# Mixer A's values: from eight narrow blocks inside the attention to three wide groups of seven half-sized products ahead of it

## The chip, the cores and the metric

One NeuronCore of one Trainium2 chip runs the whole program. The metric is the device time of one execution in microseconds (us). The kernel before takes 1451.91 us, the median of three runs (1451.7 to 1453.12).

## The reference

A two-layer encoder trunk on x of 512 positions by 1024, all in float32. Layer 0 mixes tokens with mixer A, layer 1 with mixer B (multi-head latent attention); each mixer is followed by a squared-ReLU MLP of width 4096. Mixer A is what the change touches:

```
qkv = (rms_norm(x) @ w_qkv).reshape(512, 3, 3 groups, 8 heads, 128)
for g, (window, dilation) in enumerate(((128, 1), (512, 4), (2048, 16))):
    q, k = rope(rms_norm(qkv[:, 0, g])), rope(rms_norm(qkv[:, 1, g]))
    v = qkv[:, 2, g]                       # 512 x 1024 for each g
    o_g, lse_g = dilated_window_attention(q, k, v)
o = sum_g softmax_g(lse)[g] * o_g
x = x + o @ w_o
```

So the values are three products of the 512 x 1024 activation with a 1024 x 1024 weight, one for each group.

## The kernel before, in words

**Split precision.** Each float32 weight tile comes by DMA into `raw` and is split into a high part `whi` (a copy on ScalarE, L157) and a low part `wlo` (a subtraction on VectorE, L158). The activation `hT` is split in the same way when the normalised input is transposed (L212 to L221). Each tile product is three TensorE matmuls: high by high, high by low, low by high (L184 in `run_block`). A block over 1024 of depth and 512 rows is thus 8 x 4 x 3 = 96 matmuls, into four PSUM banks named `acc`.

**Mixer A** goes by pairs of heads, b = 0 to 3. For a pair:

- `qk_block(b, g)` for g = 0, 1, 2: 96 matmuls of 512 columns (q and k of two heads). Each bank is then squared and summed on ScalarE (`junk`, L136), rotated and scaled on VectorE (L308, L311, L315, L316), transposed on TensorE (`tp`, L123), copied to `qkT` (L325). Scores follow (`sc`, L340, L344, L351), the masks from `ca`, the maximum (L359) and the exponentials (L362).
- `v_block(b, h)` for both heads: 96 matmuls of 384 columns (the three groups of one head), copied on ScalarE to `vt` (L369). Group 0 goes through a DRAM tile `vd` and comes back in two other layouts, `v0n` and `v0c`.
- `merge`: two small products `scm` (L386, L411) with a chain of small VectorE and ScalarE steps around them weigh the three groups; the weights are multiplied into the probabilities `P` (L417).
- `pv`: the probabilities are transposed (L123), copied to `pT` (L426 on VectorE, L433 on ScalarE), and multiplied with the values into `sco` (L440, L444), which goes to `oT` (L446).

In the last pair the values of one head stand ahead of the qk blocks, and those of the other after the merge. Then comes the output projection, whose first 72 matmuls need only the first heads.

**The order on each engine** comes from a scheduler that simulates the program and arranges each engine's instructions. Every engine works strictly through its own list, so an instruction that waits holds up all behind it on its engine.

**The MLPs** already use seven half-sized products per block (`wino`): a 512 x 1024 x 1024 product cut into quarters, with sums of quarters of the activation (`S`, then its split `asp`, L485 and L486) and of the weights (`wqs`), where the sum of two weight quarters is made by a DMA from GpSimd's queue that adds into SBUF (L509). A product is 24 matmuls of 512 columns (L580). `ORDER` sets their sequence: products 1, 5, 3, 6, 2, 7, 4. In the last block of an MLP (`done` given) the finished rows go on to mixer B's norm or to the output.

GpSimd has short tensor operations too, among them the tables `cgB` and `sgB` of mixer B (L691 to L693), which wait for the DMA of the gain `gr`.

Of the kernel before, what the change touches and what calls it, by code (L numbers as in the profile page):

```python
# [10 lines left out]
F32 = mybir.dt.float32  # L11
F32R = mybir.dt.float32r
AF = mybir.ActivationFunctionType
ALU = mybir.AluOpType
# [73 lines left out]
def encoder_kernel(ctx: ExitStack, tc: tile.TileContext, x, norm_mix, norm_ffn, a_w_qkv, a_q_gain, a_k_gain,  # L88
# [151 lines left out]
    oT = x16.tile([P, HA, S], F32, tag="x16", name="oT")  # L240
    with tc.tile_pool(name="apool", bufs=1, reuse_waits="tile") as ap_, \
            tc.tile_pool(name="aw", bufs=2, reuse_waits="tile") as aw, \
            tc.tile_pool(name="adram", bufs=2, space=bass.MemoryType.DRAM) as ad:
        cosg = [ap_.tile([P, NT, 2, DH], F32, name=f"cosg{g}") for g in range(NG)]
        sing = [ap_.tile([P, NT, 2, DH], F32, name=f"sing{g}") for g in range(NG)]
        xts = [aw.tile([P, D], F32, tag="vt", name=nm("xt")) for r in range(2)]
        xts += [ap_.tile([P, D], F32, tag=t, name=nm("xt")) for t in ("P00", "gqk")]

        def load_x(r):
            for hf in range(2):  # L250
                nc.sync.dma_start(xts[r][:, 512 * hf:512 * hf + 512], x_v[:, r, 512 * hf:512 * hf + 512])

        def load_w0(k):
            early[("first", k)] = load_raw(*qk_units(0, 0)[k], 512)
        cas = ap_.tile([P, 2176], F32, name="ca")
        ca = cas[:, 0:C_ALL - C_KEEP]
        load_x(0)
        gain_b = gain_table(norm_mix[0:1, :].rearrange("o d -> (o d)"), D, "g_mix0")
        nc.sync.dma_start(ck[:, 0:P], consts[:, 0:P])
        load_w0(0)  # L260
# [4 lines left out]
        load_x(3)  # L265
        nc.sync.dma_start(ca[:, 0:C_M1 - C_KEEP], consts[:, C_KEEP:C_M1])
        nc.sync.dma_start(ca[:, C_M1 - C_KEEP:], consts[:, C_M1:C_ALL])
        nc.sync.dma_start(ck[:, P:C_KEEP], consts[:, P:C_KEEP])
        for r in range(NT):
            norm_tile(r, xts[r], gain_b, hT, aw, xn_tag="qkT")  # L270
        gqk0 = ap_.tile([P, 2, 512], F32, tag="gqk", name="gqk")
# [3 lines left out]
        cosA = cc(C_COSA, C_SINA).rearrange("p (r d) -> p r d", r=NT)  # L275
        sinA = cc(C_SINA, C_M1).rearrange("p (r f d) -> p r f d", r=NT, f=2)
# [4 lines left out]
        def tables(g):  # L281

            gqk = gqk0 if g == 0 else aw.tile([P, 4, DH], F32, tag="t1", name=nm("gq"))
            for t, src in enumerate((a_q_gain, a_k_gain)):
                nc.sync.dma_start(gqk[:, t, 0:DH], src[0, g].partition_broadcast(P))
            for t in range(2):
                gb = gqk[:, t, 0:DH].rearrange("p (f d) -> p f d", f=2).unsqueeze(1)
                gb = gb.broadcast_to([P, NT, 2, 64])
                V.tensor_tensor(cosg[g][:, :, t].rearrange("p r (f d) -> p r f d", f=2),
                                cosA.unsqueeze(2).broadcast_to([P, NT, 2, 64]), gb, op=ALU.mult)  # L290
                V.tensor_tensor(sing[g][:, :, t].rearrange("p r (f d) -> p r f d", f=2), sinA, gb, op=ALU.mult)

        def qk_block(b, g, Pt, stats, first):

            qkT = aw.tile([P, 4, S], F32, tag="qkT", name=nm("qkT"))

            def evac(r, acc):
                a4 = acc.rearrange("p (c d) -> p c d", c=4)
                a5 = acc.rearrange("p (t h d) -> p t h d", t=2, h=2)
                ss = st.tile([P, 8], F32, tag="qss", name=nm("qss"))  # L300
                junk = aw.tile([P, P], F32, tag="junk", name=nm("junk"), bufs=1)
                for c in range(4):
                    mean_square(junk, a4[:, c], DH, ss[:, c:c + 1])
                t1 = aw.tile([P, 4, DH], F32, tag="t1", name=nm("t1"))
                t2 = aw.tile([P, 4, DH], F32, tag="t2", name=nm("t2"))
                t15 = t1.rearrange("p (t h) d -> p t h d", t=2)
                t25 = t2.rearrange("p (t h) d -> p t h d", t=2)
                V.tensor_tensor(t15, a5, cosg[g][:, r].unsqueeze(2).broadcast_to([P, 2, 2, DH]), op=ALU.mult)  # L308
                for hf in range(2):
                    o_ = 64 - hf * 64  # L310
                    V.tensor_tensor(t25[:, :, :, hf * 64:hf * 64 + 64], a5[:, :, :, o_:o_ + 64],  # L311
                                    sing[g][:, r, :, o_:o_ + 64].unsqueeze(2).broadcast_to([P, 2, 2, 64]),
                                    op=ALU.mult)
                rs = rstd_of(ss[:, 0:4], 4, EPS, "qrs")
                V.tensor_tensor(t1, t1, t2, op=ALU.add)  # L315
                V.tensor_tensor(t1, t1, rs.unsqueeze(2).broadcast_to([P, 4, DH]), op=ALU.mult)  # L316
                tp = tp_p.tile([P, 512], F32, tag="tp", name=nm("tp"))
                for c in range(4):
                    transpose(tp[:, c * P:(c + 1) * P], t1[:, c])
                tv = tp.rearrange("p (c t) -> p c t", c=4)  # L320
                if g == 0:
                    dst = qkT.rearrange("p c (m r) -> p c m r", r=NT)[:, :, :, r]
                else:
# [624 lines left out]
```

## Time and profile before

| what | value |
|---|---|
| median of three runs | 1451.91 us |
| time of the profiled execution | 1451.78 us |
| span of its profile | 1449.6 us, so 2.18 us lie around the span |
| mean granted clock of TensorE | 0.999 |
| TensorE matmul busy | 97% of the span, 7116 matmuls |
| VectorE, ScalarE, GpSimd busy | 61%, 50%, 14% |

A row of a group says: line, engine, operation, the tiles written and read, the count, then busy time and mean ns of one. A row of the timeline says: start, duration, engine, line, operation, and in brackets the idle time ahead of it and what ended it. In the chain of waits a row is a stretch of the chain that ended last. Matmuls overlap, so their single durations add up to more than the time that passes; the time from the start of one stretch to the next is what counts.

### The profile page before, as it was taken

Reading aid. Unit: us, or ns where it says so; the run is one execution under the profiler, and the core shown is the slowest. Engines: PE = TensorE matmul, PEld = TensorE weight load, DVE = VectorE, ACT = ScalarE, POOL = GpSimd, SP = SyncE. Lnnn points to the kernel's source line nnn. Section 1 sums busy time; section 2 is a strip of 40 time slices with the busy share of each in tenths; the row PEclk is TensorE's granted clock in tenths of the full one; section 3 lists DMA queues with packets and bytes.
Section 4 is the critical chain, followed back from the end, with each engine's and each line's share of the span. In section 5 each row is a group of like instructions: output and inputs, shape, how many; then the busy total and the mean of one; then the engine's idle time right before and its main releaser. Section 6 shows DMA issues by size and latency. Waiting matters only on the chain.

```text
span 1449.6 us, 19315 instructions
## 1 busy us (share of the span) xinstructions
PE 1410.4 (97%) x7116; PEld 1196.8 (83%) x7116; DVE 887.1 (61%) x1421; ACT 727.2 (50%) x1590; POOL 198.4 (14%) x197
## 2 busy tenths in 40 slices
PE   7999999999999999999999999899999999999998
PEld 6889889889988878888888877776768988888877
DVE  6765566566537655266475749788755266475647
ACT  5544455355335533453544545777633454544543
POOL 1120120011011101011020222332101011020210
PEclk9999999999999999999999999999999999999999
DMA  7325114321622344749394853310013749394853
GB/s 228 100 57 162 58 49 129 110 63 45 174 92 62 97 140 141 222 112 236 91 233 127 195 136 66 99 30 30 30 44 136 206 111 239 93 223 138 189 116 88
DMA packets 134813, 177.52 MB, mean 122 GB/s; under 512 B 8768, under 2 KB 73536, under 8 KB 134720
## 3 DMA queue, kind: packets, MB, share of 16 engines
q1 hardware_dynamic: 117312, 142.74, 31.1%
q0 software_dynamic: 17408, 33.56, 14.0%
q8 instruction: 56, 0.92, 0.2%
q14 instruction: 37, 0.30, 0.1%
HBM read 172.07 MB, written 4.19 MB: 122 GB/s over the span
## 4 chain that ended last, share of the span: by engine, by line
PE 89%; ACT 4%; DVE 3%; DMA 2%; issue 1%; POOL 1%; SPq 0%; DVEq 0%; ACTq 0%; POOLq 0%
PE acc L184 58%; PE sc L580 10%; PE tp L580 7%; PE tp L123 4%; PE acc L859 1%; PE acc L835 1%; PE sc L753 1%; PE sco L444 1%; PE sco L440 1%; PE sc L351 1%; PE sc L835 1%; ACT whi L157 1%; ACT junkb L136 1%; DVE wlo L158 1%; PE tp L859 0%
## 5 line engine op out<-in xcount | busy, mean ns | idle before, releaser
L184 PE MATMUL acc<-whi,hT 128*128 128x512 f32 (+2 forms) x1600 | 486.3, 379 | 5.6 <-DVE t L311 2.2
L158 DVE TENSOR_TENSOR wlo<-raw,whi 128x1024 fp32r<-128x1024 f32 (+3 forms) x170 | 195.7, 1156 | 230.5 <-ACT whi L157 229.5
L184 PEld LDWEIGHTS acc<-whi,hT 128*128 128x128 f32 x1600 | 296.2, 189 | 47.3 <-issue 2.9
L184 PE MATMUL acc<-hT_f,whi 128*128 128x512 f32 (+1 forms) x1152 | 319.4, 366 | 1.9 <-DVE resid L641 1.2
L157 ACT ACTIVATE whi<-raw 128x1024 fp32r<-128x1024 f32 (+3 forms) x170 | 170.0, 1005 | 269.0 <-PE acc L184 177.4
L184 PE MATMUL acc<-wlo,hT 128*128 128x512 f32 (+2 forms) x800 | 300.2, 375 | 0.2 <-DVE wlo L158 0.2
L184 PEld LDWEIGHTS acc<-hT_f,whi 128*128 128x128 f32 x1152 | 208.4, 189 | 37.8 <-DVE resid L641 1.6
L524 DVE TENSOR_TENSOR wlo<-wqs,whi 128x1024 fp32r<-128x1024 f32 x112 | 137.3, 1227 | 113.6 <-ACT whi L523 113.5
L184 PE MATMUL acc<-hT_f,wlo 128*128 128x512 f32 (+1 forms) x576 | 205.1, 365 | 0.0
L523 ACT ACTIVATE whi<-wqs 128x1024 fp32r<-128x1024 f32 x112 | 118.6, 1060 | 167.6 <-PE acc L184 66.2
L184 PEld LDWEIGHTS acc<-wlo,hT 128*128 128x128 f32 x800 | 151.2, 189 | 20.5 <-DVE wlo L158 1.1
L580 PE MATMUL sc<-whi,asp 128*128 128x512 f32 x512 | 165.1, 390 | 0.8 <-ACT asp L485 0.8
L509 POOL DMA_DIRECT2D wqs<-in_ffn_w_dram x64 | 77.6, 1350 | 528.4 <-DVE wlo L524 339.9
L184 PEld LDWEIGHTS acc<-hT_f,wlo 128*128 128x128 f32 x576 | 108.6, 189 | 17.5
L131 POOL TENSOR_TENSOR qrs<-rs_v,nhalf 128x4 f32<-128x4 f32 x48 | 61.5, 1290 | 408.3 <-DVE rs_v L128 393.8
L580 PE MATMUL tp<-whi,asp 128*128 128x512 f32 x352 | 112.2, 390 | 2.6 <-DVE asp L486 2.6
L580 PEld LDWEIGHTS sc<-whi,asp 128*128 128x128 f32 x512 | 96.1, 188 | 21.6 <-ACT asp L485 1.6
L580 PE MATMUL sc<-wlo,asp 128*128 128x512 f32 x256 | 99.6, 389 | 0.0
L580 PEld LDWEIGHTS tp<-whi,asp 128*128 128x128 f32 x352 | 65.9, 188 | 17.2 <-DVE asp L486 3.5
L580 PE MATMUL tp<-wlo,asp 128*128 128x512 f32 x176 | 68.5, 389 | 0.0
L136 ACT ACTIVATE junk<-acc 128x128 f32<-128x128 f32 x192 | 53.1, 277 | 18.9 <-PE acc L184 13.8
L554 DVE TENSOR_TENSOR resid<-resid,sc 128x512 f32<-128x512 f32 x64 | 43.0, 682 | 24.4 <-PE sc L580 24.4
(190 smaller groups left out, 1796.3 us busy)
## 6 DMA issues: line engine op xcount, KB each, us to landing
wqs<-in_ffn_w_dram SPq DMA_DIRECT2D x80, 512.0 KB, 5.1
raw<-in_ffn_w_dram SPq DMA_DIRECT2D x64, 512.0 KB, 4.4
wqs<-in_ffn_w_dram POOLq DMA_DIRECT2D x64, 512.0 KB, 7.2
raw<-in_a_w_qkv_dram SPq DMA_DIRECT2D x96, 256.0 KB, 3.4
raw<-in_a_w_qkv_dram SPq DMA_DIRECT2D x64, 192.0 KB, 2.8
raw<-in_a_w_o_dram SPq DMA_DIRECT2D x8, 512.0 KB, 4.0
raw<-in_b_w_o_dram SPq DMA_DIRECT2D x8, 512.0 KB, 3.7
xt<-in_x_dram SPq DMA_DIRECT2D x8, 256.0 KB, 5.7
```

What stands on the lines that cost most here:

```text
L123: PE.transpose(o, i, ident)
L131: G.tensor_tensor(out, v[:, :n], nhalf[:, :n], op=ALU.pow)
L136: A.activation(junk, x, AF.Square, scale=1.0 / math.sqrt(dim), accum_out=out)
L157: A.activation(hi[:, :nk, :n], raw[:, :nk, :n], AF.Copy)
L158: V.tensor_tensor(lo[:, :nk, :n], raw[:, :nk, :n], hi[:, :nk, :n].bitcast(F32), op=ALU.subtract)
L184: PE.matmul(accs[o][:, oc], lhsT=lt, rhs=rt, start=(kt == 0 and p_i == 0 and hv == 0), stop=(kt == total - 1 and p_i == 2), skip_group_che ...
L509: nc.gpsimd.dma_start(t, src, accum_op=ALU.add)
L523: A.activation(hi, x, AF.Copy)
L524: V.tensor_tensor(lo, x, hi.bitcast(F32), op=ALU.subtract)
L554: V.tensor_tensor(sl, sl, banks[t], op=op)
L580: PE.matmul(bk[t], lhsT=lt, rhs=rt[:, j], start=(first and k == 0 and i_ == 0), stop=(k == 3 and i_ == 2), skip_group_check=True)
L835: PE.matmul(sc, lhsT=lt, rhs=rt, start=(i == 0), stop=(i == 4))
```

## The change

- A new `v_phase` stands right behind the first qk block (pair 0, group 0). For each group it makes all 1024 value columns by seven half-sized products in the sequence 1, 2, 5, 3, 6, 7, 4, as 24 matmuls of 512 columns each (3 x 7 x 24 = 504). The results collect in `vo` and go to a DRAM tile `vall` per group; `v_load` brings what a pair needs back, ten DMAs per pair.
- The weights come as whole quarters (`b11`, `b21`, `b12`, `b22`, `bT`). Their sums are made by adding DMAs on GpSimd's queue (four sums for group 0, two for groups 1 and 2) and otherwise by VectorE.
- The sums of activation quarters `Ssp` (four of them) are made once, from the unsplit copies `h32` and `stg`, while the input is normalised.
- The eight `v_block`s, their `vt` copies and the round trips through `vd` go. The qk blocks follow one another, with the first block's q and k tables read from `rot` and the masks `ca` loaded after the value phase. The buffer `qkT` alternates between two pools.
- In the last block of each MLP product 2 moves from fifth to second place (`ORDER_LAST`).

```
+    def v_phase(vp):
+        h32 = vp.tile([P, 2, KD, P], F32, name="h32")
...
+        def add_block(t, g, ki, ni):
+            for u in range(2):
+                nc.gpsimd.dma_start(t[:, 2 * u:2 * u + 2], wblk(g, ki, ni, u), accum_op=ALU.add)
...
+                A.activation(stg[0, i], tvs[0], AF.Copy)
+                V.tensor_tensor(stg[1, i], h32[:, i, 0:4], stg[0, i], op=ALU.subtract)
+                V.tensor_tensor(stg[0, i], stg[0, i], tvs[1], op=ALU.subtract)
...
+        qk_proj(0, 0, qkT0, first_homes, lambda: jk, first=True)
+        def split_s(n, x, i):
+            hi, lo = (Ssp[n][:, :, c, i * P:(i + 1) * P] for c in range(2))
+            A.activation(hi, x, AF.Copy)
+            V.tensor_tensor(lo, x, hi.bitcast(F32), op=ALU.subtract)
...
+        def product(p, w, banks, first, u, t, parts):
+            if (p, u) not in parts:
+                parts[p, u] = split_w(w[:, 2 * u:2 * u + 2])
+            hi, lo = parts[p, u]
+            for j in range(2):
+                k = 2 * u + j
+                ah, al = A_OF[p](k, 0, t), A_OF[p](k, 1, t)
+                for i_, (lt, rt) in enumerate(((ah, hi), (ah, lo), (al, hi))):
+                    PE.matmul(banks[t], lhsT=lt, rhs=rt[:, j], start=(first and k == 0 and i_ == 0),
+                              stop=(k == 3 and i_ == 2), skip_group_check=True)
...
+            for p, w, bk in ((1, b11, ba), (2, b21, bd)):
+                for u, t in ALONE:
+                    product(p, w, bk, True, u, t, parts)
+            put(0, 0, "set", ba, False)
+            put(0, 0, "add", bd, True)
+            for u in range(2 if g else 0):
+                us = slice(2 * u, 2 * u + 2)
+                V.tensor_tensor(bT[:, us], b11[:, us], b12[:, us], op=ALU.add)
+            bb = new_banks("b")
+            for u, t in ALONE:
+                product(5, bT, bb, True, u, t, parts)
+            put(1, 1, "set", bb, False)
+            add_block(bT, g, 1, 1)
...
+            for u, t in ALONE:
+                product(6, bT, ba, False, u, t, parts)
+            put(0, 1, "sub", ba, True)
+            add_block(bT, g, 1, 0)
...
-        def v_block(b, h, vd):
-            vt = aw.tile([P, NT, NG, DH], F32, tag="vt", name=nm("vt"))
...
-            units = [(w7[:, k:k + 2, 2, :, 2 * b + h, :], 2, NG) for k in range(0, KD, 2)]
-            run_block(units, [1] * 4, 384, act_stationary(hT, 384), evac)
...
-                qk_all()
-                vs = [v_all(0), v_all(1)]
-                merge(stats, Pt, False)
...
+            vs = v_load(b)
+            for g in range(NG):
...
+                scores(b, g, qkT, Pt, stats)
+            merge(stats, Pt)
...
-        for p, chain, first, (i, n, op) in ORDER:
+        for p, chain, first, (i, n, op) in ORDER if done is None else ORDER_LAST:
...
+    ORDER_LAST = [ORDER[0], ORDER[4]] + ORDER[1:4] + ORDER[5:]
```

What this moves, at three places. A name with a number is a tile and its buffer.

**VectorE, the start of the program.** Before, as the last rows of the input are split (`hT`) and the first qk block is rotated (`t`):

```order
L221 TENSOR_TENSOR hT_91<-tp_212,hT_91 128x4x128
L221 TENSOR_TENSOR hT_91<-tp_219,hT_91 128x4x128
L308 TENSOR_TENSOR t_59_296<-acc_243,cosg_104 128x512
L311 TENSOR_TENSOR t_60_297<-acc_243,sing_107 128x4x64 x2
L128 TENSOR_SCALAR rs_v_301<-qss_290 128x4
L308 TENSOR_TENSOR t_66_343<-acc_244,cosg_104 128x512
L311 TENSOR_TENSOR t_67_344<-acc_244,sing_107 128x4x64 x2
```

The same place now, where the last bank of the same block (`t_61`) is done only thirty-odd rows further on (`h_109` is the copy `h32`):

```order
L355 TENSOR_TENSOR stg_210<-h_109,stg_210 128x512
L356 TENSOR_TENSOR stg_210<-stg_210,tp_203 128x512
L267 TENSOR_TENSOR t_46_296<-acc_247,cosg_103 128x512
L270 TENSOR_TENSOR t_46_296<-acc_247,sing_104 128x4x64 x2
L128 TENSOR_SCALAR rs_v_300<-qss_291 128x4
L370 TENSOR_TENSOR Ssp_114<-stg_210,Ssp_114 128x4x128
L370 TENSOR_TENSOR Ssp_112<-stg_210,Ssp_112 128x4x128
L274 TENSOR_TENSOR t_46_296<-t_46_296 128x512
L128 TENSOR_SCALAR rs_v_345<-qss_336 128x4
L374 TENSOR_TENSOR stg_210<-stg_210,h_109 128x512
L275 TENSOR_TENSOR t_46_296<-t_46_296,qrs_302 128x512
L346 TENSOR_TENSOR hT_91<-tp_222,hT_91 128x4x128
```

The sums `stg` and their splits `Ssp` now stand between the steps of the qk block. On TensorE the transposes of `t_61` stand ahead of the first matmul of product 5.

**TensorE, `pv` of the first pair.** Before, between the values (`sco`) and the transposes of the probabilities (`tp`), with matmuls of the pair's value and next qk blocks (`acc`) in between:

```order
L440 MATMUL sco_1352<-pT_1329,vt_999 128x128
L440 MATMUL sco_1352<-pT_1336,vt_999 128x128
L184 MATMUL acc_1428<-whi_1495,hT_91 128x512
L184 MATMUL acc_1429<-whi_1495,hT_91 128x512
L184 MATMUL acc_1429<-wlo_1496,hT_91 128x512
L184 MATMUL acc_1429<-whi_1495,hT_91 128x512 x2
L184 MATMUL acc_1429<-wlo_1496,hT_91 128x512
L444 MATMUL sco_1352<-pT_1343,v0n_1133 128x4x32
L123 MATMUL tp_1370<-ck,P_230 128x128 x2
```

Now, at the same place:

```order
L610 MATMUL sco_1934<-pT_1911,vt_1314 128x128
L610 MATMUL sco_1934<-pT_1918,vt_1314 128x128
L123 MATMUL tp_1920<-ck,P_1305 128x128 x4
L123 MATMUL tp_1927<-ck,P_1305 128x128 x4
L614 MATMUL sco_1934<-pT_1925,v0n_1317 128x4x32
L123 MATMUL tp_1952<-ck,P_1308 128x128 x4
L614 MATMUL sco_1934<-pT_1932,v0c_1318 128x4x32
L614 MATMUL sco_1934<-pT_1925,v0n_1317 128x4x32
```

From the second `scm` to the last `sco` no matmul of a qk block stands among them any more, in this pair and the next two.

**TensorE, the end of the last pair's scores.** Before, around the first of the two merge products (`scm`), with matmuls of the output projection (`acc`):

```order
L184 MATMUL acc_4990<-whi_4993,hT_4858 128x512
L184 MATMUL acc_4990<-wlo_4994,hT_4858 128x512
L386 MATMUL scm_4681<-ca,xsel_4678 128x4 x4
L184 MATMUL acc_4987<-whi_4993,hT_4858 128x512 x2
L184 MATMUL acc_4987<-wlo_4994,hT_4858 128x512
L184 MATMUL acc_4988<-whi_4993,hT_4858 128x512 x2
```

Now:

```order
L184 MATMUL acc_4738<-whi_4801,hT_4606 128x512
L517 MATMUL sc_4548<-qkT_4327 128x128
L517 MATMUL sc_4560<-qkT_4327 128x128
L517 MATMUL sc_4548<-qkT_4327 128x128
L517 MATMUL sc_4560<-qkT_4327 128x128
L555 MATMUL scm_4575<-ca,xsel_4572 128x4 x4
L580 MATMUL scm_4596<-ca,xsel_4572 128x4 x2
L123 MATMUL tp_4607<-ck,P_3800 128x128 x4
```

The 72 matmuls of the projection now all stand ahead of the last scores, and nothing stands between the last scores and the two merge products.

More of the change, by code (lines that the diff above doesn't have):

```diff
@@ L293, in qk_block @@
[L293 to L323, printed above, removed]
-                    dst = qkT[:, :, r * P:(r + 1) * P]
-                A.activation(dst, tv, AF.Copy)
-            run_block(qk_units(b, g), [4] if first else [1] * 4, 512, act_stationary(hT, 512), evac,
-                      name="first" if first else None)
```

248 lines of the change are left out of this document (190 added, 58 removed).

## The prediction

> **What bounds the kernel now.** I read the page's busy times first, then the chain of waits for the whole run.
>
> ```profile
> PE 1410.4 (97%) x7116; PEld 1196.8 (83%) x7116; DVE 887.1 (61%) x1421; ACT 727.2 (50%) x1590; POOL 198.4 (14%) x197
> PE 89%; ACT 4%; DVE 3%; DMA 2%; issue 1%; POOL 1%; SPq 0%; DVEq 0%; ACTq 0%; POOLq 0%
> ```
>
> TensorE works almost all the time, and 89% of the chain that ended last is its own work. So each microsecond of matmuls taken away counts, unless something else then ends late. What that could be is read stage by stage. The table by stage says where TensorE already waits in mixer A:
>
> ```profile
> 30.00:80.00 50.00, 50.00 (x252) 42.04 (x251) 38.38 (x76) 31.35 (x110) 10.47 (x9) 1.00 0.27 83
> 80.00:130.00 50.00, 47.76 (x273) 45.58 (x272) 29.96 (x52) 23.96 (x70) 6.00 (x4) 0.97 0.37 106
> 130.00:180.00 50.00, 50.00 (x288) 43.84 (x287) 29.07 (x56) 19.61 (x50) 4.37 (x4) 1.00 0.28 84
> 480.00:530.00 50.00, 46.56 (x272) 42.26 (x271) 35.54 (x67) 26.61 (x77) 4.84 (x4) 1.00 0.35 107
> ```
>
> The columns are TensorE, its weight loads, VectorE, ScalarE and GpSimd busy, then the granted clock. TensorE has no gap in the middle pairs; VectorE is busy for 29 to 38 us of 50. It has room on the average, but the first 50 us of real work (30 to 80) leave it only 11.6.
>
> **1. The matmuls of the values.** The pitch of a matmul is the length of an unbroken stretch in the chain of waits over its count. A stretch of value blocks alone (384 columns), and one of 512 columns:
>
> ```profile
> 117.82 14.56 PE acc L184 x84
> 841.40 18.83 PE acc L184 x83
> ```
>
> That is 14.56/84 = 0.1733 us and 18.83/83 = 0.2269 us. Removed: 8 blocks x 96 = 768 matmuls, 768 x 0.1733 = 133.1 us. Added: 504 x 0.2269 = 114.4 us. Difference **-18.7 us**, all of it on the engine that sets the end. [...]
>
> **2. The start.** The new sums and splits of activation quarters and the splits of the value weights stand on VectorE among the first qk block's steps, and the transposes of that block's last bank stand on TensorE ahead of product 5. VectorE's pitch of a 512-wide step, a 1024-wide split and the rest is read here:
>
> ```profile
> 10.47 1.23 DVE L158 TENSOR_TENSOR wlo<-raw,whi 128x1024 fp32r<-128x1024 f32 x1 [1.65 <-ACT whi L157]
> 11.61 0.68 DVE L221 TENSOR_TENSOR hT<-tp,hT 128x512 fp32r<-128x512 f32 x1
> ...
> 18.53 1.28 DVE L221 TENSOR_TENSOR hT<-tp,hT 128x512 fp32r<-128x512 f32 x2
> ...
> 32.09 0.75 DVE L311 TENSOR_TENSOR t<-acc,sing 128x256 f32<-128x256 f32 x2
> 32.76 0.16 DVE L128 TENSOR_SCALAR rs_v<-qss 128x4 f32<-128x4 f32 x1
> ```
>
> Start to start, a split takes 1.14 us and a pair of L311 0.67; of two 512-wide steps in 1.28 us the second adds 0.60. From the split that begins at 18.53 (its place in the list is the same in both) up to the last step of that bank the new list has 38 steps of 512, four pairs, nine splits, one normalisation (about 1.2) and small ones (0.6): 22.8 + 2.7 + 10.3 + 1.8 = 37.6 us. So the bank is done at 56.1 us at the earliest, if VectorE never waits. TensorE meanwhile has 144 matmuls of 512 columns and 11 groups of transposes to do. Before, it had done as many here:
>
> ```profile
> 49.87 0.44 PE tp L123 x4
> 50.31 0.70 PE acc L184 x3
> ```
>
> That is at 51.0, so it would stand idle for 5.1 us or more. VectorE waits now and then for ScalarE and GpSimd, so I take **+6.0** (5 to 9). This also says what covers the sums: nothing does, VectorE has no slack here.
>
> **3. Inside the value phase.** A product takes 24 x 0.2269 = 5.4 us of TensorE. VectorE needs two splits and two or three result steps, 2.3 + 1.2 to 1.8 us, so it keeps up, and ScalarE (two copies of 1.06) too. Groups 1 and 2 add four 1024-wide sums (4.6 us per group) ahead of products 5 and 7. The adding DMAs are priced by the page's row of such transfers (count, size, us to landing):
>
> ```profile
> wqs<-in_ffn_w_dram POOLq DMA_DIRECT2D x64, 512.0 KB, 7.2
> ```
>
> The sum for product 6 is issued behind the split for 5 and needed 10.9 us after 5 begins, with 3 between; the MLPs run these three in the same sequence without a wait on TensorE that shows. At a group's change a quarter arrives behind the last splits of the group before. **+2.5** for all three groups: the lower bound is 0 (the MLPs), the upper 6.8, a split's 1.14 at each of two changes of group and ahead of 5 and 7 in two groups; I take two to three of these six, since the sums are queued among splits that run one product ahead.
>
> **4. `pv` of the first three pairs without matmuls to fill it.** The last pair of before is the nearest row, for there hardly any stand in it:
>
> ```profile
> 521.99 0.50 PE L411 MATMUL scm<-ca,xsel 128*128 128x4 f32 x4
> 525.75 0.66 PE L123 MATMUL tp<-ck,P 128*128 128x128 f32 x4 [2.09 <-DVE pT L426]
> 532.23 0.66 PE L123 MATMUL tp<-ck,P 128*128 128x128 f32 x4 [0.29 <-DVE pT L426]
> ```
>
> In the pairs before it the same steps have cover: the window 130 to 180 shows TensorE busy throughout. Each of three pairs takes on 2.09 + 0.29 = 2.4 us: **+7.2**. Below, 0 if the scaling of `P` is done in time; above 13.8, if the six matmuls that still stood in the second head (1.2) and one result wait (1.0) come on top in each.
>
> **5. The last pair's merge.** The first product of the merge waits for the maxima of the last scores, the second for exponentials and weights. Before, VectorE and ScalarE went through this chain under matmuls of the projection and the last value block:
>
> ```profile
> 503.54 1.05 PE L351 MATMUL sc<-qkT 128*128 128x128 f32 x8
> 504.41 1.29 DVE L356 TENSOR_TENSOR P<-sc,ca 128x512 f32<-128x512 f32 x2 [1.01 <-PE sc L351]
> 505.62 0.68 DVE L656 TENSOR_TENSOR hT<-oT,hT 128x512 fp32r<-128x512 f32 x1
> ...
> 506.81 0.68 DVE L656 TENSOR_TENSOR hT<-oT,hT 128x512 fp32r<-128x512 f32 x1
> ...
> 508.01 1.89 DVE L656 TENSOR_TENSOR hT<-oT,hT 128x512 fp32r<-128x512 f32 x3
> 510.01 0.40 ACT L362 ACTIVATE P<-P,stat 128x128 f32<-128x128 f32 x1 [1.71 <-DVE stat L360]
> 513.11 1.05 ACT L157 ACTIVATE whi<-raw 128x1024 fp32r<-128x1024 f32 x1
> 514.06 0.21 ACT L397 ACTIVATE me<-me 128x24 f32<-128x24 f32 x1
> 514.19 1.23 DVE L158 TENSOR_TENSOR wlo<-raw,whi 128x1024 fp32r<-128x1024 f32 x1 [1.77 <-ACT whi L157]
> 516.40 0.49 DVE L406 TENSOR_TENSOR xsel<-me,ca 128x128 f32<-128x128 f32 x2
> ```
>
> From the end of the scores (504.6) to the second product's operand (516.9) it took 12.3 us. Five L656 steps (3.0) ahead of the exponentials and a copy and a split of weights (2.1) behind them lay within; without these it is 7.2. Now all of it stands open, since the projection's 72 matmuls come ahead of it: **+8** (7.2 to 12.3), nearer to the lower end because those L656 steps are needed by the 72 matmuls and so are done before.
>
> **6. The clock.** After the one idle time of over 2 us in the middle of mixer A the granted clock falls:
>
> ```profile
> 93.67 0.41 PE L184 MATMUL acc<-whi,hT 128*128 128x384 f32 x1 [2.24 <-DVE t L311]
> 95.00:100.00 5.00, 5.00 (x21) 5.00 (x20) 5.00 (x10) 1.10 (x5) 2.93 (x2) 0.66 0.54 150
> ```
>
> 21 matmuls ran there in 5 us, against 5/0.1733 = 29 at the full pitch, so 1.4 us are lost. After the 2.09 us at 525.75 nothing is lost that the profile shows. The open stretch of part 5 is longer than either: **+1.5**, with 0 to 6 should `pv` and the start lose it too. [...]
>
> **7. The last block of the MLPs.** In layer 0 GpSimd's adding DMAs for product 6 now stand behind `cgB` and `sgB`, which wait for `gr`:
>
> ```profile
> 860.25 3.62 DMA gr<-in_b_q_gain_dram
> ...
> 872.89 6.32 DMA wqs<-in_ffn_w_dram
> ```
>
> ```profile
> 875.20 1.26 POOL L509 DMA_DIRECT2D wqs<-in_ffn_w_dram  x1
> ```
>
> ```profile
> 865.00:870.00 5.00, 3.50 (x15) 2.55 (x15) 5.00 (x6) 1.06 (x1) 5.00 (x6) 1.00 0.01 2
> 870.00:875.00 5.00, 4.57 (x20) 3.49 (x19) 4.92 (x5) 4.01 (x4) 5.00 (x5) 1.00 0.15 6
> ...
> 895.00:900.00 5.00, 3.98 (x22) 3.14 (x21) 4.95 (x6) 2.55 (x4) 0.56 (x2) 1.00 0.00 0
> ```
>
> Before, the tables held up DMAs of product 4 alone, and TensorE lost 1.5 + 0.4 + 1.0 = 3 us in this stage. Now both DMAs of product 6 go out at 875.2, land 6.3 later and are copied (1.1) by 882.6, while TensorE, which ends its last L184 stretch at 860.2 and has products 2, 5 and 3 ahead (16.3), is there at 876.5: it waits 6.1. The difference is 3, and some of it comes back since products 7 and 4 then find all ready: **+2** (0 to 5). In layer 1 no such tables stand in the way. Product 5's operand came late after product 1:
>
> ```profile
> 1412.92 0.73 PE L580 MATMUL tp<-whi,asp 128*128 128x512 f32 x2 [1.14 <-DVE asp L486]
> ```
>
> Product 2 needs no sum and fills that time: **-1.5** (-3 to 0). The removed `vt` copies, the `vd` round trips and the later `ca` load lie under matmuls and count nothing; the ten loads of `v_load` have a pair's 90 us to land.
>
> **The sum.** -18.7 + 6.0 + 2.5 + 7.2 + 8 + 1.5 + 2 - 1.5 = **+7.0 us**. The profiled execution took 1451.8 (its span of 1449.6 and 2.2 around it), 0.1 under the median, so the change gives 1451.8 + 7.0 = **1458.8 us**. With all bounds low: -18.7 + 5 + 0 + 0 + 7.2 + 0 + 0 - 3 = -9.5; with all high +34.
>
> **The rivals.** A measurement can tell about 0.2% (2.9 us) from no change.
>
> *Saved matmuls carry through: faster.* The point is VectorE's lateness in `pv`. If the scheduler's neighbours leave the scaled `P` ready, part 4 is 1 instead of 7.2, and the value phase has no waits (0). Then -18.7 + 5.5 + 0 + 1 + 7.2 + 0 + 1 - 2 = -6.0, so 1446. For it: `P` for groups 1 and 2 is scaled before group 0. Against it: the 2.09 us of the last pair came in this order too.
>
> *No change.* Part 4 at half (3.6), part 2 at 5, the clock and layer 0 at nothing: -18.7 + 5 + 2 + 3.6 + 8 - 1 = -1.1, so 1450.7.
>
> *Adding DMAs late: much slower.* If the sums for products 6 and 4 land late in each group, TensorE stops six times. The second half's split for 5 ends 2.3 us after 5 begins, its sum lands 7.2 later and is split by 11.8; it is needed at 13.6. A landing of 11 would be 2 late, six times +12 on the forecast, so 1471. For it: at the start the DMA engines are at their fullest. Against it: the MLPs show no such wait.
>
> **How the numbers follow.** The forecast's case has 0.44, the faster rival 0.26, no change 0.18, late DMAs 0.12. Within the forecast's case nearly all lies over +2.9. So faster 0.26, within 0.2% 0.18, slower 0.56. The range takes in the faster rival and part of the late DMAs, **1445 to 1470 us**; the forecast's own case is 1455 to 1465.
>
> **What would show it.** In the changed profile: matmuls of the value phase at 0.227 us; an idle time of 5 us or more ahead of product 5 (about 50 to 57 us) that ends with a rotated `t`; waits for `pT` of 2 us in each pair; an open 7 to 12 us at the last pair's `scm` with a fallen clock behind it. If `pv` of the middle pairs shows no idle time, or the start keeps TensorE busy, the kernel is faster and the forecast wrong.

## The result, and the profile after

The changed kernel takes 1464.07 us (median), the kernel before in the same comparison 1451.81. The ratio is 1.008, with a 95% interval of 1.006 to 1.010: slower by 0.8%, 12.3 us. Forecast were 1458.8 us, slower with 0.56, and a range of 1445 to 1470.

One of its four executions was disturbed (2022.82 us at a granted clock of 0.653, the others 1462.87 to 1464.10), and as that was the one profiled, the profile shown here is of the same kernel run again: an execution of 1460.38 us with a span of 1458.6. The page's row of busy times and the shares of the chain:

```profile
PE 1400.9 (96%) x6852; PEld 1164.9 (80%) x6852; DVE 936.0 (64%) x1473; ACT 750.4 (51%) x1606; POOL 220.4 (15%) x213
PE 87%; DVE 5%; ACT 4%; issue 2%; DMA 1%; POOL 1%; SPq 0%; ACTq 0%; DVEq 0%; POOLq 0%
```

TensorE has 264 matmuls less and is busy for 9.5 us less (before 1410.4). But its idle time, the span less the busy time, is 1458.6 - 1400.9 = 57.7 us, against 1449.6 - 1410.4 = 39.2 before. That is 18.5 more, and the difference is the 9.0 us by which the span grew. The table by stage, in the stretches shown for before (TensorE's busy time is the first column behind the length, the granted clock the third from the right):

```profile
30.00:80.00 50.00, 43.87 (x196) 35.91 (x195) 38.37 (x56) 29.46 (x53) 14.50 (x10) 0.93 0.95 247
80.00:130.00 50.00, 49.59 (x219) 40.73 (x219) 33.52 (x33) 24.14 (x28) 4.81 (x4) 1.00 0.67 184
130.00:180.00 50.00, 49.84 (x237) 41.70 (x236) 27.08 (x33) 20.89 (x31) 4.81 (x4) 1.00 0.64 170
480.00:530.00 50.00, 41.40 (x211) 34.40 (x210) 37.94 (x81) 27.41 (x93) 5.32 (x4) 0.92 0.35 117
```

The value phase (65 to 170) is nearly full. The start and the end of mixer A have the holes, and there the clock is below 1 too. What TensorE waits for, over the whole run (total, times, longest):

```profile
PE tp L123 <- DVE xn L336: 9.1, 1, 9.1
PE scm L580 <- DVE xsel L575: 6.9, 1, 6.9
PE tp L123 <- DVE pT L596: 6.9, 7, 2.6
PE tp L123 <- DVE t L275: 5.7, 1, 5.7
PE sc L740 <- ACT whi L683: 4.2, 1, 4.2
...
PE acc L403 <- DVE vo L430: 1.0, 3, 0.4
...
PE scm L555 <- DVE P L522: 0.8, 1, 0.8
```

The first is the wait for the normalised input, which the kernel before has too (8.9 us). The next four are new or grown: the last pair's merge, `pv`, the start, and product 6 in the last block of layer 0's MLP. The longest idle time of each stands in the timeline, with what ended it (in the order of time: start, `pv`, merge, product 6):

```profile
57.26 1.08 PE L123 MATMUL tp<-ck,t 128*128 128x128 f32 x4 [5.75 <-DVE t L275]
350.02 0.66 PE L123 MATMUL tp<-ck,P 128*128 128x128 f32 x4 [2.58 <-DVE pT L596]
527.77 0.99 PE L580 MATMUL scm<-ca,xsel 128*128 128x4 f32 x4 [6.90 <-DVE xsel L575]
890.34 0.82 PE L740 MATMUL sc<-whi,asp 128*128 128x512 f32 x2 [4.23 <-ACT whi L683]
```

Behind the first and the last two the matmuls also run slower, and in the third pair's `pv` (445). The windows of 5 us around them:

```profile
55.00:60.00 5.00, 2.75 (x9) 2.39 (x10) 3.40 (x5) 1.75 (x2) 0.04 (x1) 0.50 0.98 214
60.00:65.00 5.00, 5.00 (x21) 4.06 (x20) 0.00 (x0) 1.56 (x2) 0.00 (x0) 0.86 0.82 297
350.00:355.00 5.00, 4.98 (x45) 4.98 (x46) 1.33 (x3) 1.20 (x2) 1.01 (x1) 1.00 0.00 0
445.00:450.00 5.00, 5.00 (x37) 5.00 (x37) 0.69 (x1) 0.60 (x1) 0.11 (x1) 0.79 0.00 0
525.00:530.00 5.00, 2.23 (x11) 2.26 (x12) 3.56 (x11) 1.23 (x7) 0.00 (x0) 0.50 0.03 12
530.00:535.00 5.00, 3.61 (x15) 2.54 (x14) 3.78 (x6) 0.61 (x2) 0.00 (x0) 0.50 0.00 0
890.00:895.00 5.00, 4.67 (x13) 3.69 (x14) 4.10 (x4) 3.03 (x4) 1.49 (x2) 0.66 0.51 68
```

The matmul time lost in a window is the busy time times what the clock lacks: 2.75 x 0.50 = 1.4 us at 55, 5 x 0.14 = 0.7 at 60, 1.1 + 1.8 at 525 to 535. Summed over all such windows it is **10.1 us**, against 1.7 before (the one window at 95). So the busy time has 8.4 us of lower clock in it, and the matmuls themselves saved 9.5 + 8.4 = 17.9. The account of the span is: -17.9 matmuls, +8.4 clock, +18.5 idle, together +9.0.

The matmuls of the value phase stand at the 0.227 us of the forecast's first sign or a little above it: two of their unbroken stretches give 5.44/24 = 0.2267 and 16.57/72 = 0.2301:

```profile
76.57 16.57 PE acc L403 x72
93.14 5.44 PE sc L403 x24
```

### The profile page after: what moved, and what is told of

It reads as the page before. It is cut to its first block, busy times and chain, and to the rows that moved or that the text cites. A ratio compares the mean times of both kernels' runs of the same rounds, so it can differ in the third digit from the quotient of the medians.

```text
span 2021.1 us, 18776 instructions
## 1 busy us (share of the span) xinstructions
PE 1986.6 (98%) x6852; PEld 1337.1 (66%) x6852; DVE 949.9 (47%) x1473; ACT 760.1 (38%) x1606; POOL 212.6 (11%) x213
## 4 chain that ended last, share of the span: by engine, by line
PE 97%; DVE 1%; ACT 1%; issue 0%; DMA 0%; SPq 0%; POOL 0%; ACTq 0%; DVEq 0%
PE acc L184 51%; PE sc L740 12%; PE tp L740 9%; PE acc L403 5%; PE tp L123 4%; PE tp L403 2%; PE acc L997 2%; PE sc L915 2%; PE acc L1021 2%; PE sc L403 1%; PE sco L610 1%; PE sco L614 1%; PE sc L517 1%; PE acc L740 1%; PE acc L123 1%; PE sc L997 1%
## 5 line engine op out<-in xcount | busy, mean ns | idle before, releaser
L184 PE MATMUL acc<-whi,hT 128*128 128x512 f32 (+1 forms) x1088 | 463.8, 511 | 1.8 <-ACT hT L817 1.1
L184 PE MATMUL acc<-hT_f,whi 128*128 128x512 f32 (+1 forms) x1152 | 430.6, 471 | 0.1
L184 PEld LDWEIGHTS acc<-hT_f,whi 128*128 128x128 f32 x1152 | 237.4, 215 | 107.5 <-issue 36.1
L184 PEld LDWEIGHTS acc<-whi,hT 128*128 128x128 f32 x1088 | 226.1, 210 | 118.7 <-issue 34.3
L158 DVE TENSOR_TENSOR wlo<-raw,whi 128x1024 fp32r<-128x1024 f32 (+3 forms) x138 | 165.2, 1201 | 270.0 <-ACT whi L157 249.8
L184 PE MATMUL acc<-wlo,hT 128*128 128x512 f32 (+1 forms) x544 | 277.9, 511 | 0.2 <-DVE wlo L158 0.2
L184 PE MATMUL acc<-hT_f,wlo 128*128 128x512 f32 (+1 forms) x576 | 264.6, 470 | 0.0
L740 PE MATMUL sc<-whi,asp 128*128 128x512 f32 x512 | 220.5, 506 | 0.0
L184 PEld LDWEIGHTS acc<-hT_f,wlo 128*128 128x128 f32 x576 | 124.4, 216 | 53.3 <-issue 17.2
L184 PEld LDWEIGHTS acc<-wlo,hT 128*128 128x128 f32 x544 | 113.3, 208 | 59.3 <-issue 18.8
L740 PE MATMUL tp<-whi,asp 128*128 128x512 f32 x352 | 150.5, 507 | 0.0
L740 PE MATMUL sc<-wlo,asp 128*128 128x512 f32 x256 | 129.9, 508 | 0.0
```

The source lines that it names most:

```text
L158: V.tensor_tensor(lo[:, :nk, :n], raw[:, :nk, :n], hi[:, :nk, :n].bitcast(F32), op=ALU.subtract)
L184: PE.matmul(accs[o][:, oc], lhsT=lt, rhs=rt, start=(kt == 0 and p_i == 0 and hv == 0), stop=(kt == total - 1 and p_i == 2), skip_group_che ...
L740: PE.matmul(bk[t], lhsT=lt, rhs=rt[:, j], start=(first and k == 0 and i_ == 0), stop=(k == 3 and i_ == 2), skip_group_check=True)
```

## The experiments

Times are medians; the ratio is to the kernel before on the same chip, with its 95% interval. The sums of idle time and of lost clock are made as above, each for the profiled execution. The intervals of two variants together leave some 3 us of uncertainty on the difference between them.

**The changed kernel again (e1).** No edit.

> The changed kernel once more, unaltered, for an undisturbed profile. Time 1462 to 1465 us. Theory A (the clock): the waits in mixer A add up to about what the prediction counted (start 6, value phase 2.5, values of the first three pairs 7, last merge 8), and the 5 us that are missing lie in matmuls that ran at a lower granted clock behind those waits: mean clock near 0.988, at least eight stretches of 5 us with a clock under 0.9. Theory B (the waits): the waits themselves are 5 us longer than counted, above all in the value phase or at the last merge, and stretches with a lower clock cost no more than 3 us together. Theory C (the MLPs' last blocks): these cost 5 us more than the 0.5 counted.

Measured 1464.14 us, 1.0081 [1.0065, 1.0098]. The profiled execution was the fastest of four: 1460.38 at a mean granted clock of 0.989; the other three took 1463.75 to 1465.36 at 0.987. Theory A holds: ten windows of 5 us have a clock under 0.9, and the waits in mixer A are near those forecast. A clock 0.002 lower over 1459 us is 2.9 us, of which only a part is matmul time: in the profile the mean clock of 0.989 stands for 16.0 us, and 10.1 of them are matmuls'. So by estimate some 2 of the 3.8 us by which the median lies above the profile are clock again; there is no profile of a slower execution that shows it.

**The new tail: taken out (e2), and put alone into the kernel before (e3).**

```
e2  -        for p, chain, first, (i, n, op) in ORDER if done is None else ORDER_LAST:
    +        for p, chain, first, (i, n, op) in ORDER:
e3  the reverse, in the kernel before
```

> The changed kernel with the old sequence in the MLPs' last blocks (product 2 in fifth place again). By the prediction's terms 7 (+2 in layer 0, -1.5 in layer 1) the time stays within 1 us of the changed kernel, 1463 to 1465. Theory C: the new sequence costs 4 us or more, so this kernel takes 1460 or less. If the new sequence is a gain by itself, as one that covers the wait for the split operand would be, this kernel is 2 to 4 us slower, 1466 to 1468.

> The kernel before with nothing changed but the sequence in the MLPs' last blocks (product 2 in second place). The mirror of the run above: by the prediction's terms +0.5, so 1451 to 1453. Theory C: 1455 or more. A gain by itself: 1448 to 1450.

e2: 1459.71 us, 1.0053 [1.0038, 1.0068]: the new tail costs 4.4 us. e3: 1454.55, 1.0022 [1.0012, 1.0032]: it costs 3.1 in the kernel before. Both are outside what the prediction's terms gave; e2 meets Theory C, e3 falls just short of it. The page's busy row of e3, its longest new wait, and the windows in which its clock was low:

```profile
PE 1414.0 (97%) x7116; PEld 1201.5 (83%) x7116; DVE 887.5 (61%) x1421; ACT 728.4 (50%) x1590; POOL 198.4 (14%) x197
```

```profile
PE sc L580 <- ACT whi L523: 4.4, 1, 4.4
```

```profile
525.00:530.00 5.00, 5.00 (x32) 5.00 (x32) 1.46 (x2) 1.19 (x2) 0.00 (x0) 0.66 0.58 175
880.00:885.00 5.00, 3.87 (x11) 3.12 (x12) 3.89 (x4) 3.01 (x3) 1.20 (x1) 0.66 0.53 79
935.00:940.00 5.00, 2.85 (x12) 2.12 (x11) 3.28 (x13) 4.97 (x24) 2.79 (x4) 0.87 0.30 95
940.00:945.00 5.00, 4.68 (x23) 3.81 (x22) 3.77 (x15) 4.56 (x20) 3.25 (x6) 0.79 0.01 3
1115.00:1120.00 5.00, 3.67 (x19) 3.67 (x20) 3.82 (x6) 2.05 (x4) 0.55 (x1) 0.66 1.03 376
```

The span is 1452.5, so TensorE is idle for 38.5 us, 0.7 less than before, but it is busy for 3.6 us longer with the same 7116 matmuls. The lost clock is 5.6 us instead of 1.7. These sums over the whole span hide what the tail does. So here are two stages, each cut at the same matmuls in the four profiles: layer 0's tail, from the last long stretch of L184 ahead of it to the end of one of the first stretches of L184 in mixer B, and layer 1's, from the last stretch of `sc` ahead of it to the end of the program.

| | before | e3 | e1 | e2 |
|---|---|---|---|---|
| sequence in the tail | old | new | new | old |
| layer 0, from and to | 841.40, 918.04 | 841.64, 920.37 | 850.97, 929.86 | 853.03, 928.55 |
| length, us | 76.64 | 78.73 | 78.89 | 75.52 |
| of that TensorE idle | 3.17 | 4.43 | 4.30 | 2.11 |
| layer 1, from | 1383.91 | 1387.32 | 1393.44 | 1393.38 |
| length, us | 65.69 | 65.18 | 65.16 | 65.62 |

In layer 0 the new tail costs 2.1 us (e3 against before) or 3.4 (e1 against e2): 1.3 or 2.2 of waiting, since the long wait is more than the smaller ones of ORDER that it replaces, and the rest is longer busy time, with the lower clock behind it (0.66 at 880). In layer 1 it gains 0.5. That makes 1.6 to 2.9 us, less than the medians' 3.1 and 4.4. The other windows of low clock in e3 are not the tail's: they stand behind waits of 2.09 us (`pT`, at 524.3), 2.01 (`junkb`, at 938.5) and 1.35 (`hT_f`, at 1116.3) that the profile of before has too, of the same length and with the clock at full, and the first of them comes over 300 us ahead of the tail. Why e3 lost its clock there and the kernel before did not, these profiles don't tell; all ten executions of e3 had a mean clock of 0.994 to 0.996.

**The sums at the start made later (e4).** The sums for products 3, 6 and 7 go to tiles of their own and so can be made behind the first qk block.

```
-                V.tensor_tensor(stg[1, i], h32[:, i, 0:4], stg[0, i], op=ALU.subtract)
-                V.tensor_tensor(stg[0, i], stg[0, i], tvs[1], op=ALU.subtract)
+                V.tensor_tensor(stg[1, i], stg[0, i], tvs[1], op=ALU.subtract)
...
+            V.tensor_tensor(xa, stg[1, i], h32[:, i, 0:4], op=ALU.subtract)
+            V.tensor_tensor(xb, xa, h32[:, i, 4:8], op=ALU.add)
```

> The changed kernel with the sums of activation quarters for products 3, 6 and 7 made later: they go to buffers that come free only when the first qk block's last rotated tiles are transposed, so some nine 512-wide VectorE steps leave the list ahead of that block's last step. All results are the same. If the idle time ahead of product 5 (5.7 us in the repeat of the changed kernel) is VectorE's list being too long, as term 2 has it: 9 x 0.6 = 5.4 us less, the wait nearly gone, at most 1 us of new wait ahead of product 3. The clock theory adds the 2.1 us of matmul time lost at a lower clock behind that wait: together 6 to 7 us, so 1457 to 1458. Without the clock's part 1459. Rival: the wait ends with a DMA or ScalarE (both are near full there), and then it stays: 1463 to 1465.

Measured 1460.1 us, 1.0050 [1.0032, 1.0068]; 4.0 under e1, short of the 1457 to 1459 that were expected, and only just clear of the uncertainty. The wait for `t` is gone, and this one is in its place, inside the value phase, with a loss of clock behind it too:

```profile
PE acc L405 <- DVE vo L432: 3.5, 3, 3.0
```

```profile
70.00:75.00 5.00, 3.32 (x8) 2.69 (x9) 4.74 (x6) 1.06 (x1) 0.00 (x0) 0.66 0.59 221
```

So VectorE's list is the cause of the start's wait, as the forecast had it. Half of the wait only moved: from 45 to 80 us TensorE is idle for 3.0 us where e1 has 6.1. VectorE has the same work, and is late 15 us further on.

**`pT` of groups 1 and 2 copied on ScalarE (e6).**

```
-                V.tensor_copy(pT, tp)
+                A.activation(pT, tp, AF.Copy)
```

> The changed kernel with the copies of transposed probabilities of groups 1 and 2 moved from VectorE to ScalarE, in all pairs. By term 4 TensorE waits in the values of pairs 1 to 3 because VectorE scales the probabilities of group 0 (2 x 1.2 us) ahead of those copies; ScalarE is free there. The transposes of group 0 then still wait for their own scaling: 2.6 becomes about 1.3 in each of the middle pairs, and the clock falls less often: 3 to 5 us less, 1459 to 1461. Rival: the wait is the scaling of group 0 itself, whose end TensorE needs in any case: under 1.5 us less, 1462.5 to 1464.

Measured 1458.9 us, 1.0044 [1.0029, 1.0059]; 5.2 under e1. TensorE's waits for `pT`, 6.9 us before the edit, are:

```profile
PE sco L610 <- ACT pT L596: 3.0, 4, 1.0
```

In the windows of `pv` of the first three pairs (250 to 265, 345 to 360, 440 to 455) the idle time is 1.4 + 1.1 + 0.1 = 2.6 us, where e1 has 1.5 + 2.9 + 2.9 = 7.3. So the rival, by which the scaling itself was the wait, is out. The wait is VectorE's order, in which the copy of `pT` stands behind the scaling of `P`. Since e1's profiled execution lies 3.8 us under its median, the profiles show less of these gains than the medians: e4's profiled execution took 0.5 us less than e1's, e6's 1.8.

**Matmuls to keep the clock up in the last merge (e5, e9, e12).** Extra fp32 matmuls of 512 columns whose product nobody reads, ahead of the second merge product: eight in e5 and four in e9, which read a small tile of the softmax, and five in e12, which can go right behind the first merge product. The edit of e12:

```
+                for _ in range(keep):
+                    PE.matmul(wt, lhsT=xs[:, 0], rhs=ca[:, 0:512],
+                              start=True, stop=True)
```

> The changed kernel with eight additional matmuls (8 columns of a statistic by 512 columns of the mask table, into a free PSUM bank that nobody reads) between the last pair's two merge products, where TensorE waits 6.9 us. The wait for the merge's second operand stays as long. Clock theory: TensorE has work in that stretch, the granted clock stays at or near 1.0 behind it, and the 3.6 us that were lost at half clock there come back: 2 to 3.5 us less than the changed kernel, 1460.5 to 1462. Rival (only the idle time counts, the clock rows are a matter of how the profile is taken): same time as the changed kernel, 1463.5 to 1465, or later by what the added matmuls overrun.

> The run with additional matmuls in the last pair's merge again, with four of them for eight, since eight took 8.7 us and overran the wait by 4. Four take 8 passes, 4.4 us, and end before the second merge product's operand is there. The wait of 6.9 us splits into about 2.2 and less than 1. Clock theory: the clock stays near 1.0 behind it or falls for one stretch of 3.4 us only, so 2 to 3 us less than the changed kernel, 1461 to 1462.5. Rival (the time is that of the waits alone): 1463.5 to 1465.

> The changed kernel with five extra fp32 matmuls of 8x512, whose product nobody reads, right behind the first product of the last pair's merge, so that TensorE is not idle for over 2 us ahead of the next one. Ten passes at 0.44 to 0.55 us are 4.4 to 5.5 us and end inside the wait of 6.9. Theory A (the rest of the loss is the lower clock behind idle stretches): the matmul time lost to the clock at 520 to 540 us falls from 3.6 us to under 1, and the time from 1464.1 to 1460.5-1462.5 us. Rival B (only the waits count, the clock follows other things): 1463.5 to 1465 us; later than that if the extra matmuls hold up the next select of the merge.

The clock theory missed in all three: e5 1468.7 us (1.0111 [1.0096, 1.0126]), e9 1464.74 (1.0095 [1.0080, 1.0110]), e12 1462.98 (1.0083 [1.0068, 1.0099], where e1 has 1.0081). e5 and e9 came out where the rival had them, e12 between the two. (A fall of 3.4 us, as in e9's expectation, is the one that the trace of before has at 95.0, shown further down.) The timeline of e5, then of e12:

```profile
525.23 8.73 PE L559 MATMUL keep<-ca,stat 128*8 128x512 f32 x16 [2.16 <-DVE stat L526]
533.89 0.61 PE L585 MATMUL scm<-ca,xsel 128*128 128x4 f32 x4
```

```profile
520.46 1.06 PE L555 MATMUL scm<-ca,xsel 128*128 128x4 f32 x8 [0.76 <-DVE P L522]
521.38 4.54 PE L559 MATMUL keep<-ca,xsel 128*128 128x512 f32 x10
528.40 0.61 PE L585 MATMUL scm<-ca,xsel 128*128 128x4 f32 x4 [2.49 <-DVE xsel L580]
...
531.69 0.79 PE L615 MATMUL sco<-pT,vt 128*128 128x128 f32 x2 [1.16 <-DVE pT L601]
...
535.47 2.58 PE L615 MATMUL sco<-pT,vt 128*128 128x128 f32 x14
```

e5's sixteen passes overran the gap. In e9 the eight took 5.11 us and filled it, but 2.16 us of waiting stood ahead of them, and 2.5 us of clock were lost at 520 to 540. In e12 the passes fitted, and 2.49 us of waiting remained behind them, which was enough: the clock fell again, 2.4 us lost at 520 to 540 instead of 3.6. And what was won came back as waiting. In e1 the fourteen `sco` matmuls start 14.93 us after the first merge product (534.74 - 519.81), in e12 15.01. The reason stands in VectorE's timeline of e1:

```profile
527.34 0.49 DVE L575 TENSOR_TENSOR xsel<-me,ca 128x128 f32<-128x128 f32 x2
527.75 2.49 DVE L586 TENSOR_TENSOR P<-P,me 128x512 f32<-128x512 f32 x4
530.15 0.16 DVE L581 COPY me<-scm 128x8 f32<-128x8 f32 x1
530.23 0.68 DVE L596 COPY pT<-tp 128x512 f32<-128x512 f32 x1
530.83 2.35 DVE L586 TENSOR_TENSOR P<-P,me 128x1024 f32<-128x1024 f32 x2
533.10 0.68 DVE L596 COPY pT<-tp 128x512 f32<-128x512 f32 x1
```

It works there without a break, and in e12 with the same durations. So from 527 to 534 VectorE sets the pace, and a slow TensorE costs next to nothing there. The account's 10.1 us of lost clock is right as an account, but not all of it could be won back.

**Three edits together (e7): e4, e6 and the old tail of e2.**

> The later sums, the copies on ScalarE and the old sequence in the MLPs' last blocks together, the matmuls of the value phase as in the changed kernel. If the parts add up: 1464.1 - 6.5 - 4 - 4.4 = 1449 us, 2 us under the kernel before. If the waits only move on to the next place, 1453 or more.

Measured 1452.73 us, 1.0003 [0.9994, 1.0013]: the time of the kernel before. Singly the three gave 4.0, 5.2 and 4.4 us, 13.7 in all; together 11.4. That lies between the expected 1449, had the parts added up, and the 1453 of waits that only move on. The page's busy row, and what is left of the large waits (`xsel` of the last merge, `vo` of the value phase; `pT` is as in e6):

```profile
PE 1402.0 (97%) x6852; PEld 1164.4 (80%) x6852; DVE 927.0 (64%) x1457; ACT 757.0 (52%) x1622; POOL 219.2 (15%) x213
```

```profile
PE scm L582 <- DVE xsel L577: 6.9, 1, 6.9
...
PE acc L405 <- DVE vo L432: 2.5, 3, 1.9
```

TensorE is busy for 1402.0 us of a span of 1451.4, so idle for 49.4, still 10.2 more than before, and 9.9 us of clock are lost (1.7 before).

**A unit of the output projection kept back for the last merge (e8, e10).** e7 with the third split of the projection's weights made to wait for the last `qkT`, so that its matmuls stand beside the merge. A bias of zero, made from `qkT`, ties them. e10 is the same but for the place of that zero tile `zl`, which takes the slot of a small tile that is there already.

```
+                    zl = st.tile([P, 8], F32, tag="zl", name="zl", bufs=1)            (e8)
+                    zl = st.tile([P, 8], F32, tag="nss", name=nm("zl"))               (e10)
+                    V.tensor_scalar(zl[:, 0:1], qkT[:, 3, S - 1:S], 0.0, None, op0=ALU.mult)
+                    A.activation(hi, raw, AF.Identity, bias=zl[:, 0:1], scale=1.0)
```

> The kernel of the run with three edits, and in the last pair the third weight unit of the output projection is split only when the last qk block's transposed tiles are copied (its copy takes a zero made from them as bias; results are the same). In the list the projection's first matmuls then stand between the two merge products and among the values, where TensorE waited 6.9 us and about 3 us, and no longer ahead of the last scores. By terms 5 and 6 those waits go, with the 3.8 us lost at a lower clock behind them; in their place TensorE waits some 6 us for the last block's tiles ahead of the scores. Together 3 to 7 us less than the run with three edits, 1446 to 1450, under the kernel before. Rival: the wait ahead of the scores is as long as what it replaces, 1452 to 1454.

> As e8_held_unit, instruction for instruction on TensorE and VectorE, but the zero bias sits in a slot that an existing small tile already had, so no later tile moves in SBUF. Theory A (e8 lost its 15 us because 32 more bytes shifted the tiles behind, and the matmuls of the MLPs then stand 0.2335 us apart instead of 0.2268): the pitch is 0.2268 again, and the time 1450 to 1455 us, what e7_three took (1452.7) or up to 3 less for the held unit. Rival B (the held unit's order itself is slow): 1466 to 1469 us again, with the pitch at 0.2335.

e8: 1468.15 us, 1.0124 [1.0107, 1.0141]. e10: 1452.57, 1.0001 [0.9991, 1.0010]. In e10 the wait for `xsel` is gone, and the scores ahead of the merge wait instead:

```profile
PE sc L521 <- ACT qkT L286: 4.6, 4, 2.5
PE tp L123 <- DVE t L277: 3.4, 2, 2.8
```

Its idle time is 1451.2 - 1401.6 = 49.6 us, e7's 49.4. So the held unit brings nothing: the matmuls that filled the merge are the ones that had filled the last scores. What cost e8 its 15 us is something else, and the next run is for that.

**A tile of 32 bytes that nobody uses (e11).** e7 with `zl` as in e8, set to zero once; no other instruction differs.

```
+                zl = st.tile([P, 8], F32, tag="zl", name="zl", bufs=1)
+                V.memset(zl, 0.0)
```

> As e7_three, with one 32-byte tile more that is set once to zero and that nobody reads; the order is the same but for that one instruction. Theory A (addresses): the pitch in the MLPs is 0.2335 us and the time 1465 to 1469 us, 13 to 16 above e7_three. Rival B (the order of e8 was slow, the addresses cost nothing): 1451 to 1455 us, as e7_three.

Measured 1469.89 us, 1.0130 [1.0115, 1.0145], 17.2 above e7. The page's busy row of e11, then stretches of one MLP block in the chain of waits, of e7 and of e11:

```profile
PE 1420.6 (97%) x6852; PEld 1164.2 (79%) x6852; DVE 926.8 (63%) x1458; ACT 757.5 (52%) x1622; POOL 218.7 (15%) x213
```

```profile
678.91 40.57 PE acc L184 x179
```

```profile
683.02 41.77 PE acc L184 x179
```

The pitch is 40.57/179 = 0.2266 us in e7 and 41.77/179 = 0.2334 in e11, at a granted clock of 1.00 in both: 3% on the matmuls of the MLPs. e8 has the same 41.77 us for 179, and e10 40.57. In mixer A, ahead of the MLPs, the longest stretch of 37 takes 8.40 us in e7 and in e11. The idle time is 48.0, no more than e7's 49.4. So e11's loss, and e8's, comes with the place of the tiles behind `zl` in SBUF and not with the order. Which tile it is was not tried.

## Why the prediction was right in sign, and where it was short

**The side and its reason held.** The forecast's case was that the matmuls saved come back as TensorE waiting for VectorE at the start, in `pv` and in the last merge. All three waits are in the profile, with the releasers named (`t`, `pT`, `xsel`). e4 and e6 take VectorE's work out of the way at two of them and win 4.0 and 5.2 us by their medians.

- *Matmuls*, -18.7: measured -17.9, 0.8 from the sum by the trace's pitches.
- *Start*, +6.0: the wait is 5.75.
- *Value phase*, +2.5: 1.0. TensorE has no wait for a sum that an adding DMA makes, the rival with 1471.
- *`pv`*, +7.2: 7.3 by windows. That it should be one price in three pairs was not so: 1.5, 2.9, 2.9.
- *Last merge*, +8: 6.90 + 0.76 ahead of its two products. The five L656 steps were done before, as argued.
- *Tails*, +2 and -1.5, thus +0.5: **short in size**. By the stages of e1, e2 and e3, layer 0's costs 2.1 to 3.4 us, part of it clock, and layer 1's gains 0.5, not 1.5: together 1.6 to 2.9. Product 6 waits 4.2 in place of the 6.1 worked out. By the medians the tail costs 3.1 (e3) to 4.4 us (e2); what lies beyond the stages is not explained.
- *Clock*, +1.5: **the step that failed.** It was priced as one fall behind the last merge. In the profile it is +8.4, outside the term's own bounds (0 to 6), and the median executions have a lower clock still. The forecast counted the long stretch of part 5 and left the others within its bounds (0 to 6); in truth the start loses 2.1, one `pv` 1.4, the last merge 3.6, layer 0's tail 1.6, mixer B 1.4. What the runs showed in its place is that waits of 2.01 and 2.09 us (e3), 2.24 (before), 2.58 (e2) and 4.23 to 6.90 (e1) had a fall behind them, in e3 even one of 1.35, and the change trades matmuls for such waits.

A gain that the forecast did not count offset part of this: the idle time of 2.24 us at 93.67 of before, with its 1.7 of clock, went with the `v_block`s, and mixer B waits 2.5 us less:

```profile
905.00:1100.00 195.00, 183.88 (x899) 141.09 (x898) 139.18 (x378) 124.82 (x400) 41.70 (x59) 1.00 0.15 46
```

```profile
915.00:1110.00 195.00, 186.36 (x911) 145.25 (x910) 139.68 (x380) 125.41 (x402) 40.09 (x59) 0.99 0.15 47
```

(the first of before, the second of e1). It is not the tail: from the matmul at which layer 0's stage above ends to the end of the wait for `hT_f` (1.35 us, in e3 at 1116.3) it takes 194.0 us in e1 and in e2, but 195.8 before and 196.0 in e3. Why it waits less was not followed up.

**Which waits bring a fall.** Whether a wait brings a fall is not fixed. The same wait of 2.58 us ahead of `pv` (350.02 in e1, 349.35 in e2) left the clock at 1.00 in e1, and in e2's profile there stands behind it:

```profile
350.00:355.00 5.00, 5.00 (x33) 5.00 (x32) 0.44 (x1) 1.20 (x2) 1.01 (x1) 0.66 0.00 0
```

33 matmuls of `pv` instead of 45, 1.7 us lost. The fall of before, behind its 2.24 us, can be read finer in its trace. From 95.0 to 98.4 us the granted clock is 0.50, with 1.00 in the tenths of a us up to 95.0 and from 98.5 on:

```profile
95.00:98.40 3.40, 3.40 (x12) 3.40 (x11) 3.40 (x7) 1.10 (x5) 1.33 (x1) 0.50 0.61 171
```

Ten matmuls of 384 columns take the 3.20 us from 95.22 to 98.42, 0.32 each where the full pitch is 0.1733. Half of 3.40 us is 1.7, the loss of the whole window at 0.66. These runs show no length of a wait that decides: behind 2.09 us the clock was at 0.66 in e3 and at 1.00 before (525 to 530), and behind 2.58 us at 0.66 in e2 and at 1.00 in e1. Priced at those 1.7 us each, the start (5.75 us) and layer 0's tail (4.23) would have added 3.4 us to the forecast's clock term; e1 lost 2.1 and 1.6 there.

**Sum.** By the profile the parts are -17.9 + 18.5 + 8.4 = +9.0 where the forecast had -18.7 + 24.2 + 1.5 = +7.0: too much waiting by 5.7, too little clock by 6.9. The two misses nearly cancel, so that the number came so near is in part luck. Of the 5.3 us by which the median came out higher (1464.07 for 1458.8), 3.7 are what the usual execution takes beyond the profiled one, and 1.6 are what is left of these terms in the profiled one.

**What stays open.** How much of the +8.4 us of clock the time would get back if the clock stayed up isn't shown: the runs that tried it (e5, e9, e12) won nothing that is clear of the uncertainty. Which of the waits of 2 to 3 us lose their clock in a given execution can't be foretold from these runs. What about the place of the tiles makes matmuls slower in e11 was not tried further. No version faster than the kernel before was found; the last merge's 6.9 us of waiting is the largest piece left in e7, and e10 shows that the matmuls at hand only move it.

## What to carry to other kernels

An engine that is 97% busy hides the chains of the others; work taken from it pays only where those chains have slack, so price the waits that the removed work covered before the saving itself. Price each new wait on TensorE at its length and, if it is like those that brought a fall here (2.01 to 5.75 us, once 1.35), as what it may cost, at the 1.1 (e4) to 2.4 us (e12) of lost clock behind it (3.6 around the 6.9 us of the merge), unless another engine sets the pace there (e12). And when an experiment adds a tile, look first at the pitch of unbroken matmuls: it may have moved everything behind it (0.2266 to 0.2334 us in e11).

## What the runs showed of the hardware

- A wait far shorter than the merge's can bring a fall: windows at 0.66 with 5 us busy (1.7 us lost) stand behind waits of 2.09 us (e3), 2.24 (before, where the trace has 0.50 from 95.0 to 98.4) and 2.58 (e2), and behind 1.35 us in e3 the clock is at 0.66 too. Behind 6.9 us (e1) it is at 0.50 for two windows.
- 32 more bytes per partition ahead of other tiles made the MLPs' matmuls 3% slower (0.2266 to 0.2334 us) at full clock, 17 us in all (e11 against e7), and the same zero tile in an existing slot cost nothing (e10).
- One matmul of 512 columns on plain fp32 tiles (the `keep` of e12, not split into a high and a low part) is two passes in the trace. Ten passes took 4.54 us at full clock, 0.45 each and so 0.91 for the matmul, four times the 0.227 of one of the kernel's own matmuls.
